# Second mixer: all low parts of the weights on GpSimd

## The chip, the cores and the metric

The kernel runs on one core of a Trainium2 chip. The metric is the device time of one execution in microseconds. A core has five engines with a queue of instructions each: TensorE (PE, with its weight loads PEld), VectorE (DVE), ScalarE (ACT), GpSimd (POOL) and SyncE (SP), which here issues the weight DMAs. An engine works off its own queue in order and waits on semaphores for the others.

## The reference

Two decoder layers on 256 tokens of width 1024, in float32. Each layer is a token mixer and a squared-ReLU MLP (width 4096), each behind an RMS norm with a shift, a scale and a gate made from a conditioning vector. The first mixer is a native sparse attention, the second, which the change touches, a differential attention:

```
def diff_mixer(h, ...):
    q, k, v = split(h @ w_in)                      # 3 x 1024 columns
    q = rope(rms_norm(q per head of 64)); k = rope(rms_norm(k per head of 64))
    p = softmax(causal(q k^T / 8))                 # 8 heads, 2 maps each
    a = p[:, 0] - lam * p[:, 1]
    o = rms_norm(a @ v, subln_g) * (1 - lam_init)
    return o @ w_out
```

## The kernel before

**Products in two parts.** PE multiplies in the short float format fp32r, so each operand is a high part (the value rounded) and a low part (what the rounding left), and each product is three matmuls: high by high, low by high, high by low (mm3, L81 to L83). Activations are split by the helper split (L76, L77). Weights come as tiles of 128x1024 float32 (512 KB, called units), and do_unit splits each: ACT casts the high part wh (L202), and another engine subtracts it from the raw tile wr to make the low part wl (L209). Which engine does that is chosen by a list, halves, through whose entries the units go in turn:

```
hi, lo = halves[0][pos["split"] % len(halves[0])]
...
step = n if lo is vec else 256
with tc.high_priority(-50):
    for c in range(0, n, step):
        cs = slice(c, min(n, c + step))
        lo.tensor_tensor(l[:, cs], r[:, cs], h[:, cs].bitcast(F32), op=ALU.subtract)
```

On VectorE the subtraction is one instruction of 1024 columns, on GpSimd four pieces of 256.

**The second mixer.** The first four units (first key half, dk) are split while the MLP before ends, all on VectorE. Then come 28 units, four each of: first query half, second key half, second query half, two value halves (dv) and two halves of the output weights (do). use(u) splits up to six units ahead of the product that needs them; raw tiles are fetched eight ahead by SP. A projection (proj_rows) takes its four units one after the other, 12 matmuls of 128x512 for each; PE waits for pieces of a low part as it comes to them.

Between the units are woven, by hand-written strings of steps and by a scheduler that orders each engine's queue: a head norm for each query and key half (head_norms: squares on ACT L807, sums on DVE L808 and L308, the reciprocal root on ACT L309 and L310 with a correction on DVE L311 to L314, the multiply L817, the rope products and sums L784, L787, L788, and transposes on PE L796), and for each of eight heads the scores (L1010, L1011, with the masked row minimum L1017 on DVE), the exponentials on ACT (L1362), the difference of the two maps on DVE (L1368 to L1372), transposes (L1378), values (L1385 to L1387), and the last norm: sums on ACT (L1391), DVE (L1393), a power on POOL (L1394, tile dnr), the multiply by it on DVE (L1397), transposes (L1402) and the split of the result (L1404 on ACT, L1405 on DVE).

Buffers of 128x1024 come from one pool of 32 for raw, high and low parts and for other tiles; a buffer is reused when its readers are done.

Of the kernel before, what the change touches and what calls it, by code (L numbers as in the profile page):

```python
# [42 lines left out]
def body(ctx: ExitStack, tc: tile.TileContext, a):  # L43
    nc = tc.nc
    vec, act, pool, pe = nc.vector, nc.scalar, nc.gpsimd, nc.tensor
# [22 lines left out]
    def z4():  # L68
        return w4("z4", F32R).rearrange("p (i s) -> p i s", i=4)
# [21 lines left out]
    halves = [[(act.copy, vec)]]  # L91
# [1236 lines left out]


    look[0], ahead_dma[0] = 6, 8  # L1330
    halves[0] = [(act.copy, pool), (act.copy, vec)]
    o4 = [(z4(), z4()) for _ in range(2)]


# [173 lines left out]
```

## Time and profile before

| | |
|---|---|
| median of 3 runs | 710.43 us (709.24 to 710.75) |
| the profiled execution | 710.62 us, span 708.8 us |
| PE, DVE, ACT, POOL busy | 678.1 (96%), 464.1 (65%), 399.5 (56%), 271.0 us (38%) |
| 402 to 510 us (second mixer): PE, DVE, ACT, POOL busy | 103.15, 81.27, 74.28, 54.06 us of 108 |
| DMA engines busy in that stretch | 0.34 to 0.49 of their time |
| granted TensorE clock there | full in every slice |

A timeline row gives the start in the span, the length, the engine, the line, the operation, output<-inputs, the shape and how many instructions are merged into it; in brackets stands the idle time of the engine before it and what ended it. A wait is put down to what came last.

### The profile page before, as it was taken

The page shows a single profiled execution, that of the slowest core. Times are in us where ns is not written, and L with a number is a line of the kernel's source. Part 1 is how long each engine was busy: PE and PEld are TensorE (multiplying, and loading weights), DVE is VectorE, ACT ScalarE, POOL GpSimd, SP SyncE. Part 2 cuts the span into 40 slices and gives each one's busy share as a digit, 9 for nine tenths or more (in the row PEclk, how much of TensorE's full clock was granted, in tenths as well). Part 3 has the DMA queues.
Part 4 walks back from the last instruction along what each step waited for, and adds up shares of the span by engine and source line. Part 5 has one row for each costly group of instructions (what it writes and reads, how often), then busy time and mean ns, then how long its engine had stood idle before and what let it go on. Part 6 is the DMA issues. An engine that isn't in the chain of part 4 may idle for free. (4 is left out here: it accounts for less than half of the span.)

```text
span 708.8 us, 11840 instructions
## 1 busy us (share of the span) xinstructions
PE 678.1 (96%) x4263; PEld 561.6 (79%) x4263; DVE 464.1 (65%) x915; ACT 399.5 (56%) x779; POOL 271.0 (38%) x302
## 2 busy tenths in 40 slices
PE   8899798999999999999999999999989999999997
PEld 6678574766789988998897687677779988998896
DVE  4346978866878497858774877867684673333533
ACT  6545537777666345634553765786576345534550
POOL 3203611001202476455552567344311384335740
PEclk9999999999999999999999999999999999999999
DMA  9999999623747889989899264343755588655001
GB/s 252 334 314 385 300 344 283 178 87 97 234 145 265 281 298 346 363 269 334 288 319 358 92 193 146 132 120 96 236 174 179 187 293 292 211 175 178 1 1 59
DMA packets 105422, 156.68 MB, mean 221 GB/s; under 512 B 6135, under 2 KB 60180, under 8 KB 105364
## 3 DMA queue, kind: packets, MB, share of 16 engines
q1 hardware_dynamic: 103952, 153.60, 66.6%
q0 software_dynamic: 1248, 2.20, 1.0%
q8 instruction: 33, 0.54, 0.3%
q14 instruction: 25, 0.20, 0.1%
q10 hardware_dynamic: 164, 0.14, 0.1%
HBM read 154.86 MB, written 1.06 MB: 220 GB/s over the span
## 5 line engine op out<-in xcount | busy, mean ns | idle before, releaser
L209 POOL TENSOR_TENSOR wl<-wr,wh 128x256 fp32r<-128x256 f32 x224 | 228.2, 1050 | 292.6 <-ACT wh L202 243.8
L209 DVE TENSOR_TENSOR wl<-wr,wh 128x1024 fp32r<-128x1024 f32 (+1 forms) x136 | 176.5, 1311 | 77.1 <-ACT wh L202 65.7
L202 ACT CAST wh<-wr 128x1024 fp32r<-128x1024 f32 x192 | 191.4, 1032 | 54.8 <-POOL wl L209 20.5
L81 PE MATMUL acc<-wh,z 128*128 128x512 f32 (+1 forms) x320 | 127.5, 398 | 0.0
L83 PE MATMUL acc<-wh,z 128*128 128x512 f32 (+1 forms) x320 | 125.3, 392 | 1.2 <-DVE z L77 1.2
L82 PE MATMUL acc<-wl,z 128*128 128x512 f32 (+1 forms) x320 | 125.1, 391 | 0.0
L81 PE MATMUL sc<-hh,wh 128*128 128x256 f32 x384 | 109.0, 284 | 0.0
L83 PE MATMUL sc<-hh,wl 128*128 128x256 f32 x384 | 108.7, 283 | 0.0
L82 PE MATMUL sc<-hl,wh 128*128 128x256 f32 x384 | 108.7, 283 | 0.0
L1206 ACT ACTIVATE t<-sc 128x512 f32<-128x512 f32 x32 | 19.2, 599 | 106.4 <-PE sc L83 106.3
L235 DVE SCALAR_TENSOR_TENSOR acc<-wr,cond,acc 128x1024 f32<-128x1024 f32 x49 | 72.9, 1488 | 7.1 <-DMA wr<-in_w_ada_dram 6.4
L81 PEld LDWEIGHTS sc<-hh,wh 128*128 128x128 f32 x384 | 73.6, 192 | 1.3 <-issue 0.8
L82 PEld LDWEIGHTS sc<-hl,wh 128*128 128x128 f32 x384 | 73.7, 192 | 0.4
L83 PEld LDWEIGHTS sc<-hh,wl 128*128 128x128 f32 x384 | 73.6, 192 | 0.0
L83 PEld LDWEIGHTS acc<-wh,z 128*128 128x128 f32 x320 | 60.1, 188 | 14.3 <-DVE z L77 2.0
L81 PEld LDWEIGHTS acc<-wh,z 128*128 128x128 f32 x320 | 60.2, 188 | 13.7 <-issue 1.9
L82 PEld LDWEIGHTS acc<-wl,z 128*128 128x128 f32 x320 | 60.2, 188 | 11.5 <-issue 0.6
L82 PE MATMUL acc<-wl,hh 128*128 128x512 f32 (+1 forms) x160 | 60.4, 377 | 2.9 <-DVE wl L209 2.9
L81 PE MATMUL acc<-wh,hh 128*128 128x512 f32 (+1 forms) x160 | 62.5, 393 | 0.0
L77 DVE TENSOR_TENSOR z<-t,z 128x512 fp32r<-128x512 f32 x24 | 20.1, 839 | 62.6 <-ACT z L76 62.6
L83 PE MATMUL acc<-wh,hl 128*128 128x512 f32 (+1 forms) x160 | 60.0, 375 | 0.0
L81 PE MATMUL sc<-wh,hh 128*128 128x256 f32 (+1 forms) x152 | 43.8, 289 | 2.1 <-DVE hh L1166 2.1
(286 smaller groups left out, 1101.9 us busy)
## 6 DMA issues: line engine op xcount, KB each, us to landing
wr<-in_w_ada_dram SPq DMA_DIRECT2D x80, 512.0 KB, 6.4
wr<-in_w_mlp_in_dram SPq DMA_DIRECT2D x64, 512.0 KB, 5.1
wr<-in_w_mlp_out_dram SPq DMA_DIRECT2D x64, 512.0 KB, 4.7
wr<-in_diff_w_in_dram SPq DMA_DIRECT2D x24, 512.0 KB, 5.6
wr<-in_w_ada_dram SPq DMA_DIRECT2D x32, 256.0 KB, 7.2
wr<-in_nsa_w_in_dram SPq DMA_DIRECT2D x16, 512.0 KB, 7.4
wr<-in_nsa_w_out_dram SPq DMA_DIRECT2D x16, 256.0 KB, 10.6
wr<-in_diff_w_out_dram SPq DMA_DIRECT2D x8, 512.0 KB, 3.8
```

Source lines behind the costliest of these rows:

```text
L77: vec.tensor_tensor(l, src, h.bitcast(F32), op=ALU.subtract)
L81: pe.matmul(out, x[0], w[0], start=start, stop=False, skip_group_check=True)
L82: pe.matmul(out, x[0], w[1], start=False, stop=False, skip_group_check=True)
L83: pe.matmul(out, x[1], w[0], start=False, stop=stop, skip_group_check=True)
L202: hi(h, r[:, 0:n])
L209: lo.tensor_tensor(l[:, cs], r[:, cs], h[:, cs].bitcast(F32), op=ALU.subtract)
L235: vec.scalar_tensor_tensor(st["acc"], r, c, st["acc"], op0=ALU.mult, op1=ALU.add)
L1206: act.activation(r, bk, AF.Relu)
```

## The change

The list of the second mixer loses its VectorE entry, so that each of the 28 units of that mixer has its low part made on GpSimd in four pieces; the list is set anew for the end of the mixer and for the MLP, as before.

```
     look[0], ahead_dma[0] = 6, 8
-    halves[0] = [(act.copy, pool), (act.copy, vec)]
+    halves[0] = [(act.copy, pool)]
     o4 = [(z4(), z4()) for _ in range(2)]
```

GpSimd's queue from the mixer's start on (kz are the cleared key buffers, wl the low parts, dnr the powers of the heads, in the order of the heads):

```order
 L834 MEMSET kz 64x2x256 x8
-L209 TENSOR_TENSOR wl<-wr,wh 128x256 x44
+L209 TENSOR_TENSOR wl<-wr,wh 128x256 x88
+L1394 TENSOR_TENSOR dnr<-dnm,nhalf 128x2
+L209 TENSOR_TENSOR wl<-wr,wh 128x256 x4
+L1394 TENSOR_TENSOR dnr<-dnm,nhalf 128x2
+L209 TENSOR_TENSOR wl<-wr,wh 128x256 x8
+L1394 TENSOR_TENSOR dnr<-dnm,nhalf 128x2
+L209 TENSOR_TENSOR wl<-wr,wh 128x256 x4
 L1394 TENSOR_TENSOR dnr<-dnm,nhalf 128x2 x2
```

The rows without a sign stand in both; before, the two powers that end this piece are the first two heads', and one unit and the third head's power follow. Now 22 units stand ahead of the first power, one between first and second, two between second and third.

VectorE's queue in the head norm of the first key half (the rope sums go back into qn; hns are the sums of the next norm):

```order
 L784 TENSOR_TENSOR ropeA<-qn,csg 128x256
 L784 TENSOR_TENSOR ropeB<-qn,csg 128x256
-L209 TENSOR_TENSOR wl<-wr,wh 128x1024
 L787 TENSOR_TENSOR qn<-ropeA,ropeB 128x16x8
 L788 TENSOR_TENSOR qn<-ropeA,ropeB 128x16x8
-L209 TENSOR_TENSOR wl<-wr,wh 128x1024
 L808 TENSOR_REDUCE hns<-t 128x8 x2
 L308 TENSOR_SCALAR hnm<-hns 128x16
```

The two units that stood among the steps of the norm are gone; the steps themselves keep their order here.

VectorE's queue about the third head's multiply (pr are scores, dmn their row minima, here of the seventh head, z the split result):

```order
 L1372 SCALAR_TENSOR_TENSOR pr<-pr,dcf 128x256
-L209 TENSOR_TENSOR wl<-wr,wh 128x1024
+L1017 ISA pr,dmn<-sc,consts 128x128
+L1017 ISA dmn 128x1
+L1405 SCALAR_TENSOR_TENSOR z_4479<-tr,subg,z_4478 128x256
 L1393 SCALAR_TENSOR_TENSOR dnm<-dss,dcf 128x2
-L1405 SCALAR_TENSOR_TENSOR z_4479<-tr,subg,z_4478 128x256
+L1017 ISA pr,dmn<-sc,consts 128x128
+L1017 ISA dmn 128x1
 L1397 TENSOR_SCALAR qn<-tr,dnr 128x128 x2
```

One unit is gone, and two of the four row minima, which all stood behind the multiply L1397, now stand ahead of it.

## Rows read from the trace of the kernel before

**Rows 1.** Waits of PE, 402 to 510 us: engine, line, releaser: total, times, longest.

```profile
PE tr L1402 <- DVE qn L1397: 1.4, 3, 1.0
PE tr L1378 <- DVE z L1405: 1.3, 1, 1.3
PE tr L796 <- DVE qn L788: 1.1, 2, 0.6
PE sc L1010 <- DVE dmn L1017: 0.9, 1, 0.9
```

**Rows 2.** Groups in the mixer: count | busy us, mean ns | idle before, releasers.

```profile
L209 POOL TENSOR_TENSOR wl<-wr,wh 128x256 fp32r<-128x256 f32 x56 | 48.7, 901 | 33.4 <-ACT wh L202 27.8 <-issue 5.6
L209 DVE TENSOR_TENSOR wl<-wr,wh 128x1024 fp32r<-128x1024 f32 x14 | 19.5, 1401 | 4.3 <-ACT wh L202 4.3
```

**Rows 3.** Timeline of POOL: start, length, line, operation, count, idle before.

```profile
404.02 15.01 POOL L209 TENSOR_TENSOR wl<-wr,wh 128x256 fp32r<-128x256 f32 x16 [5.56 <-issue]
...
414.82 0.91 POOL L209 TENSOR_TENSOR wl<-wr,wh 128x256 fp32r<-128x256 f32 x1
...
416.57 1.71 POOL L209 TENSOR_TENSOR wl<-wr,wh 128x256 fp32r<-128x256 f32 x1
...
460.53 2.82 POOL L209 TENSOR_TENSOR wl<-wr,wh 128x256 fp32r<-128x256 f32 x4 [3.90 <-ACT wh L202]
```

**Rows 4.** Timeline of DVE, head norm of the first key half, POOL at its pieces.

```profile
410.56 0.18 DVE L311 TENSOR_TENSOR hnt<-hnr 128x16 f32<-128x16 f32 x1 [0.53 <-ACT hnr L310]
...
412.83 1.29 DVE L817 TENSOR_TENSOR qn<-acc,hnr 128x512 f32<-128x512 f32 x2
414.16 0.98 DVE L784 TENSOR_TENSOR ropeA<-qn,csg 128x256 f32<-128x256 f32 x1
...
418.36 0.83 DVE L788 TENSOR_TENSOR qn<-ropeA,ropeB 128x128 f32<-128x128 f32 x1
```

**Rows 5.** Timeline of DVE, head norm of the first query half.

```profile
424.31 0.18 DVE L311 TENSOR_TENSOR hnt<-hnr 128x16 f32<-128x16 f32 x1 [2.60 <-ACT hnr L310]
...
425.20 1.29 DVE L817 TENSOR_TENSOR qn<-acc,hnr 128x512 f32<-128x512 f32 x2
426.52 0.50 DVE L784 TENSOR_TENSOR ropeA<-qn,csg 128x256 f32<-128x256 f32 x1
...
428.57 0.28 DVE L788 TENSOR_TENSOR qn<-ropeA,ropeB 128x128 f32<-128x128 f32 x1
```

**Rows 6.** Timeline of ACT, casts of high parts.

```profile
401.37 1.08 ACT L202 CAST wh<-wr 128x1024 fp32r<-128x1024 f32 x1
...
410.44 3.89 ACT L202 CAST wh<-wr 128x1024 fp32r<-128x1024 f32 x4
...
424.18 1.98 ACT L202 CAST wh<-wr 128x1024 fp32r<-128x1024 f32 x2
...
452.51 1.99 ACT L202 CAST wh<-wr 128x1024 fp32r<-128x1024 f32 x2
...
474.79 1.04 ACT L202 CAST wh<-wr 128x1024 fp32r<-128x1024 f32 x1
```

**Rows 7.** Timeline of PE, transposes that end three head norms.

```profile
429.00 1.07 PE L796 MATMUL tr<-first,qn 128*128 128x128 f32 x8 [0.47 <-DVE qn L788]
...
443.54 1.03 PE L796 MATMUL tr<-first,qn 128*128 128x128 f32 x8
...
457.59 1.06 PE L796 MATMUL tr<-first,qn 128*128 128x128 f32 x8 [0.62 <-DVE qn L788]
```

**Rows 8.** Timeline of DVE, end of the second query half's head norm.

```profile
456.94 0.29 DVE L787 TENSOR_TENSOR qn<-ropeA,ropeB 128x128 f32<-128x128 f32 x1
457.15 0.28 DVE L788 TENSOR_TENSOR qn<-ropeA,ropeB 128x128 f32<-128x128 f32 x1
```

**Rows 9.** Timeline of POOL, powers of the second and third head.

```profile
477.23 0.70 POOL L1394 TENSOR_TENSOR dnr<-dnm,nhalf 128x2 f32<-128x2 f32 x1 [5.32 <-DVE dnm L1393]
...
482.17 0.69 POOL L1394 TENSOR_TENSOR dnr<-dnm,nhalf 128x2 f32<-128x2 f32 x1 [1.23 <-DVE dnm L1393]
```

## Prediction

> **What bounds the kernel now.** I read the waits of TensorE (PE) in the second mixer first, then the groups of instructions there, then the timelines of the other engines one after the other. The waits [rows 1] show that PE, between 402 and 510 us, stands still for only 1.4 + 1.3 + 1.1 + 0.9 = 4.7 us, and always for VectorE (DVE). So the mixer is bound by PE's own products, and the most that any relief of DVE can give back is 4.7 us. No wait in that list is for a low part of the weights: they are made far enough ahead.
>
> The groups [rows 2] show how the low parts of the mixer's 28 weight tiles ("units", 128x1024) are made: 56 pieces of 128x256 on GpSimd (POOL), which are 14 units, and 14 whole units on DVE, 19.5 us of it. POOL's list says that it mostly waited for ScalarE (ACT) to cast the high part. After the change POOL has 112 pieces, DVE none.
>
> **What a piece costs, and whom it holds up.** Four pieces that had no DVE work of the long kind beside them took 2.82 us; sixteen that ran among DVE's whole units took 15.01 us, 3.75 per unit, and a single one of these 1.71 us [rows 3]. So POOL and DVE take turns: a piece that meets a whole unit on DVE waits for it. These whole units are what the change takes away, so I price a unit on POOL at 2.82 us, plus 0.2 us for each of the four rope operations of a head norm that fall on it (0.91 us for a piece beside one, against 2.82 / 4 = 0.71). That is 28 x 2.82 = 79 us, and with 16 rope operations 82 us, in a stretch of about 100 us. As a rate POOL keeps up.
>
> The turns work the other way too. Between 410.6 and 412.8 us, with POOL at its pieces, the four small steps after the reciprocal root (L311 to L314) took 412.83 - 410.56 = 2.27 us from the first to L817 [rows 4]; at 424.3 us, with POOL waiting, the same four took 425.20 - 424.31 = 0.89 us [rows 5]. The first rope product took 0.98 against 0.50 us, L788 0.83 against 0.28 us. Each of these has two operands in SBUF or is the kind of tensor_scalar that DVE runs fast. L817, with one operand in PSUM, took 1.29 us in both.
>
> The Trainium skill says the same as a rule that speaks against this change: in "SBUF — State Buffer", section "Who interferes with whom", a DVE instruction with two SBUF inputs or in a two-port mode and a GpSimd instruction that reads SBUF hold one pair of ports in turn, the second waiting for all of the first. By this rule a small DVE step that comes while POOL has a queue of pieces pays up to a whole piece, however short it is; 2.27 / 4 = 0.57 us a step with pieces and 0.22 us without [rows 4, 5] agree. By a reading in which the two only share bandwidth, the small steps would cost nothing and the first two terms below would be 0.
>
> **The sum, term by term.** In each head norm ACT casts weights right after it has made the root, so I count POOL's progress from the casts [rows 6]: the first unit's high part is ready at 401.37 + 1.08 = 402.45 us.
>
> 1. *Head norm of the first query half (424.3 us).* Before, POOL had nothing to do when it began. Now POOL has by then done (424.31 - 402.45 - 1.6) / 2.82 = 7.2 units of the nine whose high parts are cast (1 + 4 + 4; the first and the last of these cast rows are shown), and two more are cast at 424.18. It works on through the whole chain. L311 to L314 then cost what they cost in [rows 4]: 2.27 - 0.89 = 1.38 us more; the first rope product 0.98 - 0.50 = 0.48; L788 0.83 - 0.28 = 0.55. Sum 2.4 us. PE already waits 0.47 us at the end of this very chain [rows 7], so all of it lands on PE. Bounds: 0 (no turns) and 3.3 us (four full pieces of 0.71 in place of 0.89 us, 1.95, with the ropes 3.0, and one more piece's remainder).
> 2. *Head norm of the second query half (452 us).* Here POOL must stop: units 18 and 19 are cast only at 452.51 us [rows 6], behind the root. With seventeen units, 402.45 + 17 x 2.82 + 2.4 = 452.8 us on the clock of before-plus-2.4, it is out of work when the small steps run, so these stay cheap. But L787 and L788 took 0.29 and 0.28 us there, the price without a piece [rows 8], and now a second unit is on POOL: 2 x (0.83 - 0.28) = 1.1 us. PE waits 0.62 us on this chain too [rows 7]. Bounds 0 and 4 us (if POOL is still busy: another 1.38 for the small steps and, as an estimate from these, as much for the combine steps before them).
> 3. *The power of the third head.* The power L1394 stands in POOL's queue. Before, one unit lay between the second head's and the third's; now the twenty-third unit stands ahead of the second, and two units between second and third. Unit 23 is cast at 474.79 + 1.04 = 475.83; + 2.82 = 478.65 us for the second power, against 477.23 [rows 9]: 1.4 us late. I cost this at nothing, since PE stood 1.3 us soon after it [rows 1] for L1405, which was queued on DVE behind a whole unit that is now gone; if that cover fails it costs 1.4. Then 0.70 us for the power and 2 x 2.82 for units 24 and 25: 485.0 us for the third, against 482.17: 2.8 us late. Behind the multiply that needs it, DVE has the last two reductions of the seventh head's scores, for which ACT, DVE and PE then wait in turn. Two of the four reductions now stand ahead of it, so I count 2.2 of the 2.8. Bounds 0 and 2.8 + 0.7 = 3.5 us.
> 4. *The sixth head* gets a unit ahead of its power that was behind it before; the seventh loses one. I cost it at 0, at most half a unit, 1.4 us.
>
> PE's own work does not change. PE waits for pieces two at a time (half a unit), and is late for none by the rates above: unit 12 is ready at 402.45 + 12 x 2.82 + 2.4 = 438.7 us, and PE was through with it only at 443.54 [rows 7]. The order of DMA issues does not change; buffers that DVE read are freed by POOL a little later, while the DMA engines are half idle in the mixer, so nothing.
>
> Sum: 2.4 + 1.1 + 2.2 + 0 = 5.7 us later, carried to the end because everything behind the mixer follows PE. The profiled execution took 710.62 us, so 716.3; it lies 0.2 above the median of the runs, 710.43. Forecast 716.1 us.
>
> **The rivals.**
> - *POOL becomes the bound by rate.* If pieces stay at the 3.75 us per unit of [rows 3], the third power comes at 402.45 + 25 x 3.75 + 1.4 = 497.6 us, 15.4 late, and the time is 726 us; at the stretch's mean of 901 ns a piece [rows 2], 3.6 per unit, 722. It decides from (482.17 - 402.45 - 1.4) / 25 = 3.13 us a unit. For it: the mean of all pieces. Against it: the dear pieces are those beside DVE's whole units, which go.
> - *The relief of DVE pays for the turns.* The stalls of 0.9 and 1.3 us lie behind whole units on DVE that go; if these 2.2 us come back to PE and the late power is hidden, 2.4 + 1.1 - 2.2 = 1.3 us remain: 711.7, which cannot be told from no change. Against it: the 0.9 us lies in a stretch whose end ACT's evacuations set, not PE.
> - *Faster.* If POOL is idle again when the small steps at 424.31 come, the first term is gone, the second with it, and the 2.2 us are gained: 708.2 us. This is decided at one place: POOL would have to finish nine units in 424.31 - 402.45 us, 2.43 us a unit, below the cheapest unit seen, or two casts would have to come later than now. At the very most all 4.7 us come back: 705.7.
> - That the change does not do what it says is excluded by the order of instructions: 56 more pieces on POOL, 14 fewer units on DVE.
>
> **How the numbers follow.** Within 0.2% (1.4 us) is about what a measurement of this kernel can tell from no change. I give the forecast's mechanism, with its sum between 3 and 9 us, a chance of 0.64; POOL as the bound 0.09; a slowdown of 1.4 to 3 us, in which one of the terms is hidden, 0.08; the relief that just pays 0.11; faster 0.08. So slower 0.81, same 0.11, faster 0.08. The likeliest case alone reaches from 713.4 to 719.4. The whole range goes down to 711.0, where the relief nearly pays, and up to 720.5: the bounds of terms 1 to 4 together would be 3.3 + 4 + 3.5 + 1.4 = 12 us, 722.6, and they will not all be met at once.
>
> **What would show it.** Right: pieces start about 0.70 us apart throughout; L311 to L314 of the first query half take over 2 us, and PE waits some 3 us at L796 near 429 us in place of 0.47; the third L1394 follows twelve pieces and DVE waits for it near 485 us. PE's waits in the mixer rise from 4.7 to about 10 us. Wrong: pieces of 0.9 us on average, or PE waiting for POOL's pieces at L82 (then POOL is the bound); or L311 to L314 at under 1.2 us with POOL at work (then turns cost nothing).

## The result and the profile after

The changed kernel took 719.88 us (median of 4 runs, 718.45 to 724.08) against 710.59 for the kernel before on the same chip (709.24 to 711.99): ratio 1.0137, 95% interval 1.0112 to 1.0163. It is slower by about 9 us; forecast were 716.1, range 711.0 to 720.5. The profiled execution is the quickest of the four: 718.45 us, span 715.7, so its trace shows less than the medians differ by.

PE's waits after, 402 to 520 us; they answer to [rows 1]:

```profile
PE tr L1402 <- DVE qn L1397: 4.8, 5, 1.6
PE tr L796 <- DVE qn L788: 4.7, 2, 3.1
PE tr L1378 <- DVE z L1405: 1.7, 3, 0.9
PE tr L1378 <- DVE dnm L1393: 0.5, 1, 0.5
PE sc L1010 <- DVE dmn L1017: 0.4, 1, 0.4
PE tr L1378 <- ACT pr L1362: 0.3, 1, 0.3
```

The sum rises from 4.7 to 12.4 us. Again no line names a low part: PE never waited for POOL's pieces. POOL's group, 402 to 510 us, beside [rows 2]:

```profile
L209 POOL TENSOR_TENSOR wl<-wr,wh 128x256 fp32r<-128x256 f32 x111 | 80.5, 762 | 17.1 <-ACT wh L202 10.2 <-issue 6.9
```

A piece fell from 901 to 762 ns, since the dear ones beside whole units on DVE are gone. VectorE in the norm of the first query half after:

```profile
422.89 0.41 DVE L311 TENSOR_TENSOR hnt<-hnr 128x16 f32<-128x16 f32 x1 [3.08 <-ACT hnr L310]
423.33 0.66 DVE L312 TENSOR_TENSOR hnt<-hnt,hnm 128x16 f32<-128x16 f32 x1
...
425.48 1.29 DVE L817 TENSOR_TENSOR qn<-acc,hnr 128x512 f32<-128x512 f32 x2
426.80 0.92 DVE L784 TENSOR_TENSOR ropeA<-qn,csg 128x256 f32<-128x256 f32 x1
...
429.23 0.81 DVE L788 TENSOR_TENSOR qn<-ropeA,ropeB 128x128 f32<-128x128 f32 x1
```

From L311 to L817 it took 2.59 us where [rows 5] have 0.89; it looks like [rows 4] now. POOL's list says why: one string of 44 pieces runs across the whole norm.

```profile
401.16 31.55 POOL L209 TENSOR_TENSOR wl<-wr,wh 128x256 fp32r<-128x256 f32 x44 [4.12 <-issue]
...
454.80 6.03 POOL L209 TENSOR_TENSOR wl<-wr,wh 128x256 fp32r<-128x256 f32 x8 [4.44 <-ACT wh L202]
...
471.68 2.80 POOL L209 TENSOR_TENSOR wl<-wr,wh 128x256 fp32r<-128x256 f32 x4 [2.03 <-issue]
474.44 0.69 POOL L1394 TENSOR_TENSOR dnr<-dnm,nhalf 128x2 f32<-128x2 f32 x1
...
481.39 0.71 POOL L1394 TENSOR_TENSOR dnr<-dnm,nhalf 128x2 f32<-128x2 f32 x1
482.06 5.80 POOL L209 TENSOR_TENSOR wl<-wr,wh 128x256 fp32r<-128x256 f32 x8
487.82 0.69 POOL L1394 TENSOR_TENSOR dnr<-dnm,nhalf 128x2 f32<-128x2 f32 x1
...
502.02 2.81 POOL L209 TENSOR_TENSOR wl<-wr,wh 128x256 fp32r<-128x256 f32 x4 [3.47 <-issue]
504.79 0.69 POOL L1394 TENSOR_TENSOR dnr<-dnm,nhalf 128x2 f32<-128x2 f32 x1
505.44 3.80 POOL L209 TENSOR_TENSOR wl<-wr,wh 128x256 fp32r<-128x256 f32 x4
509.20 0.69 POOL L1394 TENSOR_TENSOR dnr<-dnm,nhalf 128x2 f32<-128x2 f32 x1
```

The five powers shown are those of the first, second, third, sixth and seventh head; each follows a unit without a gap, so it was ready before POOL was. The multiply of the third head shows what that does on VectorE, before (0.41 us of waiting for the power) and after (3.17):

```profile
482.89 0.61 DVE L1397 TENSOR_SCALAR qn<-tr,dnr 128x128 f32<-128x128 f32 x2 [0.41 <-POOL dnr L1394]
```

```profile
488.54 0.61 DVE L1397 TENSOR_SCALAR qn<-tr,dnr 128x128 f32<-128x128 f32 x2 [3.17 <-POOL dnr L1394]
```

PE at the transposes of the two query halves, beside [rows 7]:

```profile
430.19 1.07 PE L796 MATMUL tr<-first,qn 128*128 128x128 f32 x8 [3.15 <-DVE qn L788]
...
459.70 1.06 PE L796 MATMUL tr<-first,qn 128*128 128x128 f32 x8 [1.56 <-DVE qn L788]
```

To see where the time went I compare the start of the same PE instruction in two traces, counted in each from the first L796 of the first key half (419.24 us before, 417.83 after). Microseconds later than before:

| PE's instruction | after | e2 | e3 | e9 | e8 | e10 | e11 |
|---|---|---|---|---|---|---|---|
| L796, first query half | 2.60 | -0.01 | 2.59 | 2.59 | 0.99 | 0.00 | -0.01 |
| L796, second key half | 2.59 | -0.01 | 4.22 | 4.20 | 0.75 | -0.01 | -0.02 |
| L796, second query half | 3.52 | 0.91 | 5.15 | 5.12 | 1.65 | 0.90 | 0.88 |
| L1378, fourth head | 3.06 | 0.45 | 4.69 | 4.66 | 0.64 | -0.12 | -0.14 |
| L1378, fifth head | 4.13 | 1.50 | 5.18 | 5.72 | 0.61 | -0.21 | 0.57 |
| L1378, sixth head | 4.11 | 1.50 | 5.19 | 5.71 | -0.94 | -1.69 | -1.61 |
| L1378, seventh head | 6.33 | 3.72 | 5.54 | 7.93 | -0.98 | -1.73 | -2.77 |
| L1402, fifth head | 6.81 | 4.20 | 5.77 | 8.40 | -0.87 | -1.62 | -2.74 |
| L1402, sixth head | 8.24 | 5.63 | 5.62 | 8.27 | -0.88 | -1.56 | -1.98 |
| L1154, end of the mixer | 8.24 | 5.62 | 5.45 | 10.33 | -1.47 | -2.16 | -3.43 |

From this L1154 to the end of the trace both take 193.87 us. The changed kernel's trace reaches the instruction from which the table counts 1.41 us sooner than the one of before, and its span is 8.24 - 1.41 = 6.83 us longer.

### The profile page after: what moved, and what is told of

It is laid out like the page before. It is cut to its first block, busy times and chain, and to the rows that moved or that the text cites. A ratio compares the mean times of both kernels' runs of the same rounds, so it can differ in the third digit from the quotient of the medians.

```text
span 715.7 us, 11876 instructions
## 1 busy us (share of the span) xinstructions
PE 677.4 (95%) x4263; PEld 560.9 (78%) x4263; DVE 454.8 (64%) x901; ACT 399.4 (56%) x779; POOL 303.1 (42%) x358
## 5 line engine op out<-in xcount | busy, mean ns | idle before, releaser
L209 POOL TENSOR_TENSOR wl<-wr,wh 128x256 fp32r<-128x256 f32 x280 | 260.6, 964 | 281.1 <-ACT wh L202 230.4
L209 DVE TENSOR_TENSOR wl<-wr,wh 128x1024 fp32r<-128x1024 f32 x122 | 157.0, 1301 | 70.8 <-ACT wh L202 61.0
```

## The experiments

**e1, e2: the first 12 units alone, the last 16 alone.** From the kernel before, in do_unit, with the units of the other list left to take turns:

```
             hi, lo = halves[0][pos["split"] % len(halves[0])]
+            if u in sum(([U["dq", 0], U["dk", 1], U["dq", 1]]), []):   # e2: dv and do instead
+                lo = pool
```

> Half of the change: only the first 12 of the mixer's 28 units (first query half, second key half, second query half) have all low parts on GpSimd; the other 16 alternate as before. Theory (port turns in the head norms, plus powers queued behind pieces): the head norm of the first query half costs +2.7 us and that of the second query half +0.9 as in the changed kernel, and none of the later steps, so PE's transposes L1154 after the mixer come 3.6 us later than before, measured from the mixer's start: about 714. Rival A (the loss is in the powers alone): no change, 710.6. Rival B (GpSimd's rate is the bound): the first 12 units are the densest, so most of the loss, 7 to 9 us, is here: 718.

> The other half: the first 12 units alternate as before, all low parts of the last 16 on GpSimd. Theory: the first query half's head norm is as before; the powers of the first, third, fourth and sixth heads come late as in the changed kernel, together 4.6 us, and the second query half's norm may pay its 0.9 too, since unit 18 and 19 are in this half: 4.6 to 5.5 us, about 715.5. Rival A (port turns alone cost): 1 us or less, 711.5. Rival B (rate): about 1 us, since GpSimd has slack here.

e1: 714.07 us (9 runs, 712.27 to 717.34), ratio 1.0061 [1.0037, 1.0085]. e2: 715.93 us (4 runs), 1.0081 [1.0051, 1.0111]. Their excesses over the kernel before add up to 1.42%, and the change has 1.37%: within the intervals, the loss is the sum of two halves. e2's column steps at the seventh head (2.2 us) and at the sixth (1.4), as the column of after does. The size at the norm can't be read from e1's profiled execution, one of its slowest (717.33 us): there another thing happened, told below at e12.

**e3, e4: the powers on ScalarE, with and without the change.** The same edit in the changed kernel (e3) and in the kernel before (e4):

```
-            pool.tensor_tensor(r, m, nhalf.to_broadcast([P, 2]), op=ALU.pow)
+            lg = small([P, 2], "dnl")
+            act.activation(lg, m, AF.Ln)
+            act.activation(r, lg, AF.Exp, scale=-0.5)
```

> The changed kernel with the eight powers L1394 taken off GpSimd: logarithm and exponential on ScalarE in their place, so that no head waits for GpSimd's queue. Theory: what the late powers cost (4.6 us of the 8.2) goes, the 3.6 us of the two head norms stay; DVE's wait for the power becomes one for ScalarE, 0.2 to 0.6 us longer or shorter per head: 714 to 715. Rival A (the later loss is port turns in the heads' combine steps and not the powers' queue): the time stays at 719 to 720.

> The control: the kernel before with the same exchange of the powers. Theory: before, a power stood behind GpSimd's pieces at three heads, and PE's stalls for L1397 were 1.4 us in all, so at most 1.4 us are gained, and two small ScalarE steps of 0.2 us come into each head: 709 to 711. If it gains more than 2 us, the gain of the exchange in the changed kernel is not all from the queue that the change made.

e3: 715.45 us (9 runs), 1.0068 [1.0041, 1.0095]. e4: 708.91 us (10 runs), 0.9983 [0.9965, 1.0001], its mixer 1.98 us shorter in the trace, all of it behind the second query half. From the second query half on e3 loses only 5.45 - 5.15 = 0.3 us, where after loses 8.24 - 3.52 = 4.7. So 4.4 of these 4.7 us go when the powers leave POOL's queue. Not all of that is the change's: the same exchange gains 2.0 us without it, and against e4 the change still costs 0.3 + 2.0 = 2.3 us in this part. What these 2.3 us are is not shown; PE waits 1.52 us at the second head's last transposes in e3 and not at all there in e4. The 1.6 us at the second key half in e3's column were expected by neither theory; e12 has more on them.

**e5, e6: pieces of 512 and of 128 columns.** In the changed kernel, for the mixer's 28 units alone:

```
-                step = n if lo is vec else 256
+                step = n if lo is vec else (512 if u in sum([U["dq", 0], U["dk", 1], U["dq", 1], U["dv", 0], U["dv", 1], U["do", 0], U["do", 1]], []) else 256)   # e6: 128
```

> The changed kernel with the 28 units of the mixer in pieces of 512 columns on GpSimd (two a unit) instead of 256. Theory (a small VectorE step waits for the whole piece that GpSimd is at): a piece takes about 1.4 us, so L311 to L314 of the first query half take 4 x 1.3 = about 5.2 us instead of 2.6, the rope product and L788 0.7 us more each; the term at that norm grows from 2.6 to about 6.7 us, that of the second query half from 0.9 to about 2; the powers' term stays (a unit is as long as before). In all 12 to 14 us over the kernel before, about 724 us. Rival (the price is GpSimd being busy at all, or its bandwidth, or a cost per instruction): L311 to L314 stay at 2.6 us or fall, the time is 720 us or less.

> The changed kernel with the mixer's units in pieces of 128 columns (eight a unit). Theory (whole pieces are waited for): a piece takes about 0.37 us, L311 to L314 of the first query half about 1.5 us, the term there falls from 2.6 to about 1 us and that of the second query half to about 0.5; the powers' term of 4.7 us stays or grows by what the pieces cost in all: a unit of 2.82 us plus four times the fixed part of a piece, unknown, at most some 0.1 us each. In all 6 to 7 us over the kernel before, 716.5 to 718 us. Rival (busyness or bandwidth): L311 to L314 stay at 2.6 us, and the time at 720 us; rival (a fixed cost per piece is most of a piece): a unit over 4 us and the time well above 722 us.

e5: 724.66 us (4 runs), 1.0212 [1.0187, 1.0237]. VectorE at the norm of the first key half of e5:

```profile
410.78 1.22 DVE L312 TENSOR_TENSOR hnt<-hnt,hnm 128x16 f32<-128x16 f32 x1
412.04 1.22 DVE L313 TENSOR_SCALAR hnt<-hnt 128x16 f32<-128x16 f32 x1
413.29 1.22 DVE L314 TENSOR_TENSOR hnr<-hnr,hnt 128x16 f32<-128x16 f32 x1
```

A step of 0.18 us takes 1.22, and pieces of 512 start 1.26 us apart: the price of a step is the length of the piece. The place was missed, and that the time met the forecast of 724 us is luck. At the first query half POOL had just run dry (its string ended at 424.84, L311 began at 426.82), so the steps from L311 to L314 were cheap there; the loss came at the first key half, where PE now waited 2.6 us. Up to the first query half 2.6 more were lost: 1.4 while the granted clock stood at 0.50 right behind that wait (420.8 to 424.2 us), and 1.2 by a wait of 1.67 us in place of 0.47, since POOL's next string met the last rope steps.

e6: 734.41 us (4 runs), 1.0358 [1.0311, 1.0406], far above the 718 expected. The steps did as the theory says: L312 to L314 of the first query half took 0.38 us each, L311 to L817 1.57. What PE lost by them can't be read: it was 1.00 us later there, but 1.6 us had gone to a granted clock of 0.50 (423.0 to 426.4 us), and it did not wait at these transposes at all. And a piece of 128 columns starts 0.418 us after the one before it, not 0.35, so a unit costs 3.34 us, above the 3.13 from which the prediction's first rival begins; and two steps of VectorE were caught for very long (rows of e6):

```profile
407.85 9.80 DVE L308 TENSOR_SCALAR hnm<-hns 128x16 f32<-128x16 f32 x1
...
453.20 7.48 DVE L1370 SCALAR_TENSOR_TENSOR dcf<-dsm 128x2 f32<-128x2 f32 x1
```

POOL, in the same stretch of e6:

```profile
400.83 16.79 POOL L209 TENSOR_TENSOR wl<-wr,wh 128x128 fp32r<-128x128 f32 x40 [4.13 <-issue]
419.22 41.44 POOL L209 TENSOR_TENSOR wl<-wr,wh 128x128 fp32r<-128x128 f32 x96 [1.60 <-issue]
```

L308 ended at 417.65, L1370 at 460.68, POOL's strings at 417.62 and 460.66: these steps got no turn between pieces at all, but waited for the string's end. PE stood 4.7 us behind the first of them and 7.2 behind the second.

**e7: GpSimd only writes.** In the changed kernel, for the same 28 units (the list mixer):

```
+                        if lo is pool and u in mixer:
+                            if c == 0:
+                                lo.tensor_tensor(l[:, 0:2], r[:, n - 2 : n], h[:, n - 2 : n].bitcast(F32), op=ALU.subtract)
+                            for _ in range(2):
+                                pool.memset(l[:, cs].bitcast(F32), 0.0)
+                            continue
```

> The changed kernel, in which GpSimd reads two columns of a unit (one subtraction 128x2, which waits for the cast) and then only writes: eight memsets of 128x256, about 0.33 us each, so that a unit keeps it busy for about 2.9 us as before; the mixer's low parts are cleared and not computed. Theory (turns are for reading: a GpSimd instruction that only writes doesn't hold a VectorE step up): L311 to L314 of the first query half take 0.9 to 1.1 us with GpSimd busy beside them, and the term there is 0 to 0.5 us. Rival (any GpSimd instruction holds the step up for its length): 4 x 0.33 us, about 1.4 us, and the term about 1 us. Rival (GpSimd's busyness as such): 2.6 us as with pieces. The powers still wait behind units: 4 to 5 us, so 714 to 716 us by the theory, 718 to 720 by the last rival.

705.11 us (1 run), below every forecast; the mixer's low parts are not computed here, so the time is no gain. POOL was quicker than planned (memsets 0.25 us apart) and idle at the first query half, so the 0.89 us from L311 to L817 there tell nothing. The test fell to the first key half, where a string of 13 memsets ran from 408.08 to 411.42 us (L318 to L321 are L311 to L314 here):

```profile
408.75 0.18 DVE L319 TENSOR_TENSOR hnt<-hnt,hnm 128x16 f32<-128x16 f32 x1
408.96 2.50 DVE L320 TENSOR_SCALAR hnt<-hnt 128x16 f32<-128x16 f32 x1
411.50 0.18 DVE L321 TENSOR_TENSOR hnr<-hnr,hnt 128x16 f32<-128x16 f32 x1
413.09 0.43 DVE L791 TENSOR_TENSOR ropeA<-qn,csg 128x256 f32<-128x256 f32 x1
```

The steps of two SBUF operands ran at full speed among memsets (0.18 and 0.43 us against 0.66 and 0.92 among pieces); the tensor_scalar waited until the string was over. So it is reading that makes a two-operand step wait, and a tensor_scalar can wait for writing too. The Trainium skill, "SBUF — State Buffer", section "Who interferes with whom", makes just this distinction, with tensor_scalar in a two-port mode as the kind that meets any GpSimd instruction; this trace agrees on which steps wait (0.18 and 2.50 us). It differs on how long: the Trainium skill has a wait last for one instruction of the other engine, while this one lasted through some ten memsets, and the next tensor_scalar among memsets (at 418.78 us, L308 in the kernel before) took only 0.24 us.

**e8: everything on VectorE.** The list of the mixer is [(act.copy, vec)].

> The opposite change: all 28 units of the mixer on VectorE, 1024 columns each, GpSimd left with the powers. The trace of the kernel before has 1.40 us for a unit on VectorE with GpSimd beside it; alone perhaps 1.1 to 1.2 us. Theory (what GpSimd costs is turns and its queue): the small steps of all head norms run at 0.9 us and powers come at once, the stalls of 1.3 and 0.9 us behind whole units may double, VectorE has 14 x 1.2 = 17 us more work in a stretch in which it was busy for 81 of 108 us. Gain of turns 0 to 1 us in the first key half (not waited for), loss 1 to 4 us from units ahead of small steps: 711 to 714 us. Rival (VectorE becomes the bound): over 718 us. Rival (GpSimd's part was a net loss already): below 709 us.

708.74 us (10 runs), 0.9984 [0.9972, 0.9996]: a little quicker than before, as the last rival had it and not my theory. VectorE was busy for 84.97 of 108 us only (before 81.27): without POOL beside it a unit takes 1.22 us there, 1.40 in [rows 2]. Its column shows 1.65 us lost up to the second query half's norm and 3.1 gained from there on, where no unit stands ahead of a power on POOL any more.

**e9: the sixth head's power alone on ScalarE.** In the changed kernel the edit of e3 for head 5 (counted from 0) alone.

```
+            if s.h == 5:
...
+            else:
+                pool.tensor_tensor(r, m, nhalf.to_broadcast([P, 2]), op=ALU.pow)
```

> The changed kernel with the power of the sixth head alone on ScalarE (logarithm and exponential), the other seven on GpSimd as before. Theory (the sixth head's 1.4 us are its power waiting in GpSimd's queue behind a unit): the shift of PE against the kernel before stays +6.8 us up to the fifth head's last transposes and no longer steps to +8.2 at the sixth's; 6.8 us at the end of the mixer, or a little less. Rival (the step has another cause, such as VectorE's order there): it stays at +1.4 us, 8.2 at the end.

724.36 us (1 run). The step at the sixth head is gone: 8.40 to 8.27, where after goes from 6.81 to 8.24. The end is not at 6.8, as the theory had it, but at 10.33: 1.6 us came early, at the second key half (see e12), and 2.1 behind the sixth head. There the scheduler put two units ahead of the seventh head's power, 0.9 us were lost up to its transposes, and 1.2 more while the granted clock stood at 0.50 (516.8 to 520.2 us). POOL in e9:

```profile
508.19 6.57 POOL L209 TENSOR_TENSOR wl<-wr,wh 128x256 fp32r<-128x256 f32 x8 [3.45 <-issue]
514.72 0.68 POOL L1399 TENSOR_TENSOR dnr<-dnm,nhalf 128x2 f32<-128x2 f32 x1
```

**e10, e11: the first 12 units as before, the last 16 on VectorE; e11 with the powers on ScalarE.**

```
+            if u in sum([U["dv", 0], U["dv", 1], U["do", 0], U["do", 1]], []):
+                lo = vec
```

> The kernel before, in which the last 16 units of the mixer are all made on VectorE and the first 12 take turns as before, so that GpSimd's queue holds only the powers in the heads' part. With all 28 units on VectorE, PE's transposes were 1.65 us late at the second query half's norm and then gained 3.1 us up to the end of the mixer. Theory (the early loss comes from the first 12 units, the later gain from the free GpSimd): 0 at the second query half's norm and -2.5 to -3.1 us at the end, 707 to 708 us. Rival (the gain was only the early delay given back): -1.5 us at most, about 709 us.

> The same with the powers on ScalarE too. With the powers on ScalarE the kernel before ended the mixer 2.0 us earlier. Theory (both gains are the same wait, that of a power behind a unit, which is already gone with the units on VectorE): within 0.7 us of the version with powers on GpSimd, 707 to 708 us. Rival (the gains add): -4 us or more at the end of the mixer, below 706.5 us.

e10: 708.34 us (12 runs), 0.9964 [0.9946, 0.9982]. e11: 706.70 us (6 runs, 705.35 to 708.50), 0.9947 [0.9928, 0.9966]. Both beat the kernel before; e11 is the quickest here that computes everything. Each came between its theory and its rival: -2.16 us at the mixer's end for e10, and 1.3 more for e11. The 0.90 us at the second query half were expected to be 0; from there on e10 gains the 3.1 us of its theory. Waits of DVE in e10, then in e11:

```profile
DVE qn L1399 <- POOL dnr L1396: 4.7, 8, 0.9
```

```profile
DVE qn L1401 <- ACT dnr L1398: 0.5, 1, 0.5
```

In the kernel before this wait was 5.9 us, after the change 11.6. With POOL's queue empty there remain 8 x 0.6 us for the power itself and its way over and back; on ScalarE most of that goes too.

**e12: the mean (L308) on ScalarE.** In e1, e3 and e9 the profiled execution shows L308 of the first key half at 7.0 us, as in e1 (L310 is L308 there):

```profile
410.16 6.99 DVE L310 TENSOR_SCALAR hnm<-hns 128x16 f32<-128x16 f32 x1
417.69 0.18 DVE L313 TENSOR_TENSOR hnt<-hnr 128x16 f32<-128x16 f32 x1 [0.53 <-ACT hnr L312]
```

It ended when POOL's first string did (403.16 + 13.97 = 417.13), and that string ended because ACT's next casts stand behind the root, which needs L308. PE waited 2.9 us there, ahead of the point from which the table counts. In after the same step took 0.74 us. I thought this the reason of the spread of after's times. In the changed kernel:

```
+        if name == "hn" and len(halves[0]) == 1 and halves[0][0][1] is pool:
+            act.activation(m, ss, AF.Copy, scale=1.0 / w, bias=EPS)
+        else:
+            vec.tensor_scalar(m, ss, 1.0 / w, EPS, op0=ALU.mult, op1=ALU.add)
```

> The changed kernel with L308 (mean plus epsilon) of the second mixer's four head norms on ScalarE. In the profiled runs of three kernels with all early units on GpSimd, L308 of the first key half took 7.0 us, up to the very end of GpSimd's string of twenty pieces, PE waited 2.9 us at the first key half's transposes and its clock fell in the next norm; in the profiled run of the changed kernel itself it took 0.74 us. Theory (this one step lies in wait for a gap in GpSimd's string in some runs of the changed kernel and not in others, which spreads its times from 718.5 to 724.1 us): without it on VectorE there is no wait of PE at the first key half, the median is 717.5 to 719, and no run is above 721 us. Rival (any small step can be caught so): another of L311 to L314 takes several us and the times still reach 724. Rival (the spread has another cause): 719.9 us as before, spread as before.

720.76 us (6 runs, 718.47 to 725.18), 1.0155 [1.0123, 1.0187]: the theory fell. PE had no wait at the first key half, no small step was caught, and yet the times spread as before. But the profiled execution showed a second thing. Stretches of e12 from just before the transposes of the first query half (us, busy PE, PEld, DVE, ACT, POOL, then PEclk, the granted clock, DMA share, GB/s):

```profile
426.00:430.00 4.00, 0.84 (x5) 0.40 (x4) 3.73 (x5) 0.00 (x0) 4.00 (x6) 1.00 0.90 344
430.00:433.00 3.00, 3.00 (x12) 2.71 (x13) 0.00 (x0) 1.85 (x3) 2.44 (x4) 0.51 0.64 199
433.00:440.00 7.00, 7.00 (x32) 5.75 (x31) 3.64 (x7) 5.77 (x10) 6.46 (x10) 0.97 0.45 145
```

The same stretches of after:

```profile
430.00:433.00 3.00, 2.81 (x17) 2.50 (x18) 0.04 (x1) 2.09 (x3) 2.71 (x4) 1.00 0.62 180
433.00:440.00 7.00, 7.00 (x33) 5.79 (x32) 4.64 (x9) 5.90 (x10) 6.81 (x10) 1.00 0.58 202
```

In both PE had stood for 3.1 us. In e12 the granted clock then fell to 0.51, 1.2 of 2.4 GHz; in after it did not. What that costs stands in PE's rows of e12, against 1.07 and 0.48 us in after:

```profile
429.94 1.86 PE L799 MATMUL tr<-first,qn 128*128 128x128 f32 x8 [3.16 <-DVE qn L791]
431.45 0.78 PE L81 MATMUL acc<-wh,hh 128*128 128x512 f32 x1
```

In e12, as in e3 and e9, PE is then 1.6 us later at the second key half (4.24, 4.22, 4.20 against 2.59). In those two the clock fell there as well (0.51 from 433.6 us, 0.50 from 434.9). So the same stall costs 2.6 us in one execution and 4.2 in another. Behind the 2.9 us at the first key half the clock stayed full in e3 and e9 and fell in e1 (0.51 from 422.0 to 428.9 us).

## Why the prediction was right, point by point

**The sign and the mechanism** were right: two places where POOL's longer queue meets the small steps of a norm, and the queue in front of the powers. e1 and e2 separate the halves; e3 takes nearly all of the second away, though e4 shows that 2.0 us of that come without the change too; e5 to e7 show that the price of a step is a whole piece that reads, and at times more than one.

**Term 1** (first query half, 2.4 us): measured 2.60. Each part stood near its count: L311 to L817 2.59 (2.27 counted), rope product 0.92 (0.98), L788 0.81 (0.83), PE's wait 3.15 in place of 0.47.

**Term 2** (second query half, 1.1): measured 0.93. POOL had run dry as counted (it was idle from 450.36 to 454.80 us), and L311 to L817 took 0.89 us; PE's wait rose from 0.62 to 1.56. The two steps that were to be dearer were, against [rows 8]:

```profile
458.12 0.69 DVE L787 TENSOR_TENSOR qn<-ropeA,ropeB 128x128 f32<-128x128 f32 x1
458.74 0.81 DVE L788 TENSOR_TENSOR qn<-ropeA,ropeB 128x128 f32<-128x128 f32 x1
```

**Term 3** (third head's power, 2.2): the step of PE from the sixth to the seventh head's L1378 is 2.22 us, most of it in two waits of 0.91 us, at the third head's L1402 and at the seventh head's L1378, where before there was none. The cover for the second power held: PE had lost 5.37 us at the second head's L1402 and was back at 4.11 at the sixth head's L1378.

**Term 4 is the step that failed.** The sixth head, costed at 0 with 1.4 as its bound, cost 1.43: its power waited for the whole unit at 502.02 us, and nothing covered it. PE at the sixth head's transposes, before and after:

```profile
499.35 0.44 PE L1402 MATMUL tr<-first,qn 128*128 128x128 f32 x2 [0.22 <-DVE qn L1397]
```

```profile
506.18 0.44 PE L1402 MATMUL tr<-first,qn 128*128 128x128 f32 x2 [1.64 <-DVE qn L1397]
```

e9 takes just this power out of the queue and the step is gone. I had set it against a unit that the seventh head loses, and that was misread: the seventh head loses none. Before, POOL had these, the powers of the sixth and the seventh head with a unit between them, and after there is one between them too (505.44 us):

```profile
497.96 0.69 POOL L1394 TENSOR_TENSOR dnr<-dnm,nhalf 128x2 f32<-128x2 f32 x1 [4.59 <-DVE dnm L1393]
498.61 3.81 POOL L209 TENSOR_TENSOR wl<-wr,wh 128x256 fp32r<-128x256 f32 x4
502.38 0.69 POOL L1394 TENSOR_TENSOR dnr<-dnm,nhalf 128x2 f32<-128x2 f32 x1
```

PE waits 1.02 us for the seventh head's multiply in both, so nothing came back there.

**Not priced at all:** the first head's power, behind the unit at 471.68 us (likely about 0.6 us: 3.52 at the second query half, 4.11 at the sixth head's L1378, while e3, without that queue, has 5.15 and 5.19), and 0.5 us about the eighth head, whose cause I have not followed. With these 2.60 + 0.93 + 2.22 + 1.43 + 0.6 + 0.5 = 8.3 us, and the trace has 8.24. The medians differ by 9.3; where the other 1 us lies is open.

**Not foreseen:** the clock that falls after a stall of 3 us. It isn't in the profiled execution, whose clock is 1.0 throughout; the other three, at mean granted clocks of 0.990 to 0.995, took 0.8 to 5.6 us longer. That the fall at the first query half is part of it is likely from e12, e3 and e9, but no trace of those three executions shows it. A mean below 1 doesn't say where the clock fell: e4, with 0.994, has it at 0.50 at 82.8 and 202.3 us and full in the whole mixer. The spread stays open.

**The rivals.** POOL as the bound is refuted for pieces of 256 (units at 2.8 us, no wait of PE for a piece). Faster fell where the prediction had it decided: POOL was not idle at the first query half, its string ran to 432.71 us. The relief that pays did not come: the stall for L1405 did not go but rose from 1.3 to 1.7 us.

## What to carry to other kernels

Moving elementwise work to GpSimd is priced by what it does to VectorE's small steps that lie on a chain: each may have to wait for a whole GpSimd instruction (here a step of 0.18 us took 0.66 among pieces that start 0.70 us apart), and in some executions for a whole string of them. A tiny operation in the queue of an engine that holds long strings of weight work is late by what stands ahead of it: price every one of them, also those whose neighbour gets earlier. Here the better direction was the opposite one: the last 16 units on VectorE and the powers on ScalarE gave 0.9947 of the time before.

## What the runs showed of the hardware that was not expected

- A waiting step of VectorE need not get the next gap. L308 waited 7.0 us through some ten pieces of 256 columns (e1, e3, e9) or took 0.74 (after); with pieces of 128 it waited 9.8, and L1370 7.5 us (e6). Each time the wait ended with POOL's string.
- Starts of pieces lie 0.418, 0.696 and 1.255 us apart (medians of e6, after and e5) for 128, 256 and 512 columns: about 0.14 us a piece and 0.28 for each 128 columns. Shorter pieces make turns cheaper and the whole dearer.
- After the same stall of PE of 3.1 us the granted clock stayed full (after) or fell to 0.51 for about 3 us (e12, e3, e9).
